# Keys of the neighbourhood heads kept on both sides of the context's keys, with two score matmuls per block

## The chip, the cores and the metric

The kernel runs on one core of a Trainium2 chip. The metric is the device time of one execution in microseconds (us). The engines are PE (TensorE: matmuls, with PEld for its weight loads), DVE (VectorE), ACT (ScalarE), POOL (GpSimd) and SP (SyncE, which issues most DMAs).

## The reference

One layer of a diffusion backbone over 512 latent tokens (a grid of 8 rows by 64 columns) and 256 context tokens, width 1024, everything in fp32. The layer has a modulated norm, one input projection, two groups of 8 attention heads each, an output projection with a gated residual, a mixture of 16 experts, and a last norm. The change lies in the second group, the neighbourhood heads (64 wide). Each latent query sees the keys of a window of 8 by 16 grid positions, with a learned bias for each relative position, and all 256 context keys, in one softmax:

```python
s = jnp.einsum('bqhd,bjkhd->bhqjk', qr, kr).astype(jnp.float32) * scale
s = s + jnp.transpose(bias, (0, 2, 1, 3)).astype(jnp.float32)[None]
s = jnp.where(col_in[None, None, :, None, :], s, MASK_VALUE).reshape(B, H, GRID_W, kh * GRID_W)
s_ctx = jnp.einsum('bqhd,bchd->bhqc', qr, k_ctx).astype(jnp.float32) * scale
p = jax.nn.softmax(jnp.concatenate([s, s_ctx], axis=-1), axis=-1).astype(v.dtype)
```

## The kernel before, in words

The latent tokens are laid out column of the grid by column, so that a window of 16 columns is 128 neighbouring tokens, a tile. The queries are shifted by 64 tokens against the keys: a block of 128 queries needs two key tiles. Query blocks i = 0, 1 and 2 need key tiles i and i + 1; block 3, which holds both ends of the grid, needs tiles 3 and 0. Each block has 512 scores for each query: 256 of latent keys and 256 of context keys.

The heads are worked on in four pairs, p = 0 to 3, with u = 0, 1 for the head in the pair and i = 0 to 3 for the block: 32 blocks, numbered b (line 712). The keys of a head lie in the tile `kk`, 128 partitions by 768 columns: columns 0 to 511 are the four latent tiles, 512 to 767 the context. Partitions 0 to 63 hold the key rounded to fp32r, 64 to 127 the rest that rounding leaves. The queries have two operands, `qh` (rounded, twice) and `ql` (the rest), so a score is two fp32r matmuls on the same columns, added up in PSUM. The functions around the change are these.

- `na_bias` (lines 548 to 552): DVE writes two biases with their masks into `bb`, one for blocks 0 to 2 and one for block 3, whose first half is for tile 3 and second for tile 0.
- `na_part` (lines 575 to 589): brings a projection out of PSUM. For keys, ACT copies to the upper half of `kk` (line 587) and DVE subtracts into the lower half (line 589). j = 1 is the latent keys, j = 2 the context's.
- `na_scores` (lines 593 to 606): the score matmuls, lines 604 (`qh`) and 605 (`ql`). Blocks 0 and 1 have two pieces of 256 columns (window, context), four matmuls. In block 2 the tiles 2 and 3 lie next to the context, so it has one piece of 512, two matmuls. Block 3 has pieces of 128, 128 and 256 columns, six matmuls.
- `na_max` (lines 608 to 611): DVE adds the bias to the window's 256 columns in PSUM (line 610) and takes the row maximum (line 470).
- `na_exp` (lines 613 to 617): ACT's exponential with row sums.
- `na_turn` (lines 619 to 627): four transposes on PE, copied to `pt` by DVE or ACT in turn (lines 82 and 84).
- `na_values` (lines 629 to 651): the product with the values; its rows of 512 columns take their moving operand from `pt` in four runs of 128 columns.

The loop over the blocks (lines 712 to 775) writes out the order by hand: scores, maximum, one step of the next pair's projections (`pull`, lines 57 to 59), the transposes of the block before, the exponential, after every second block a part of the modulation (`mod_rest`, line 521: two loads of 512 KB of `w_mod_b` on SP's queue into three `raw` buffers, and eight matmul instructions), and more steps of the projection, counted in `NS`. In the last pair the projections pulled are those of the latent attention (values, and splits of its weights), which come through the same `raw` buffers. The framework that builds the program may put an instruction ahead of earlier ones of its engine that are not ready yet, so the order in the trace is not quite that of the text. After this stage come the latent attention and then the experts.

Of the kernel before, what the change touches and what calls it, by code (L numbers as in the profile page):

```python
# [13 lines left out]
OP = mybir.AluOpType  # L14
# [3 lines left out]
P = 128  # L18
D = 1024
KT = 8  # L20
T = 512
TC = 256
# [11 lines left out]
K_MA, K_MB, K_KC, K_KS, K_QC, K_QS = 0, 256, 512, 640, 768, 896  # L34
# [4 lines left out]
def hybrid_kernel(tc, nc, x_k, x_q, ctx, cvec, w_mod_a, w_mod_b, b_mod_c, b_mod_r, g_ffn_row,  # L39
                  w_v, w_kv, w_ql, w_qk, g_q, g_kv, w_uq, w_ukv, rel, w_out_a, w_out_b, w_r, b_r,  # L40
                  w_gate, w_up, w_down, g_fin_row, cpk0, cpk, out):
    sy, ac, ve, pe, gp = nc.sync, nc.scalar, nc.vector, nc.tensor, nc.gpsimd
# [7 lines left out]
    def f(ap):  # L50
        return ap.bitcast(F32)
# [27 lines left out]
    def copy(dst, src, of=2):  # L79
        turn[0] += 1  # L80
        if turn[0] % of == 1:
            ve.tensor_copy(dst, src)
        else:
            ac.copy(dst, src)
# [34 lines left out]
    ident = c0[:, C_ID:C_ID + P]  # L119
# [53 lines left out]
    cka = htp.tile([P, K_QC], F32, name="cka")  # L173
# [28 lines left out]
    def bank(*nums):  # L202

        n = taken[nums] = taken.get(nums, -1) + 1
        return psA.tile([P, 512], F32, name="ps", tag=f"b{nums[n % len(nums)]}", bufs=1)

    def bank4(*nums):
        return bank(*nums).rearrange("p (a b) -> p a b", a=4)
# [143 lines left out]
    for b in range(3):  # L352
        n = KB[b + 1] - KB[b]
        wh, wl = load_split(w_kv[:, KB[b] * 288:KB[b + 1] * 288], n * 288)
        for i in range(n):
            k = KB[b] + i
            s = slice(i * 288, (i + 1) * 288)
            for t in range(6):
                mm3(akv[t][:, 0:288], hh[:, k, key_cols(t)], hl[:, k, key_cols(t)], wh[:, s], wl[:, s],
                    start=(k == 0), stop=(k == KT - 1))  # L360
# [4 lines left out]
    for b in range(4):  # L365
        wh, wl = load_split(w_ql[b], 768)
        for i in range(2):
            k = 2 * b + i
            s = slice(i * 384, (i + 1) * 384)
            for t in range(4):  # L370
                mm3(aq[t][:, 0:384], hh[:, k, q_cols(t)], hl[:, k, q_cols(t)], wh[:, s], wl[:, s],
                    start=(k == 0), stop=(k == KT - 1))
# [16 lines left out]
    ks = cka[:, K_KS:K_KS + 128].rearrange("p (t d) -> p t d", t=4)  # L389
# [5 lines left out]
    for c in range(2):  # L395
        for b0, n in ((0, 4), (4, 2)):
            tr = bank4(4, 5, 6)
            for i in range(n):
                pe.transpose(tr[:, i, :], kvt[:, b0 + i, c * P:(c + 1) * P], ident)
            s = slice(b0 * P, (b0 + n) * P)  # L400
# [4 lines left out]
    for b0, n in ((0, 4), (4, 2)):  # L405
        tr = bank4(4, 5, 6)
# [10 lines left out]
    for c in range(3):  # L417
        tr = bank4(4, 5, 6)
# [48 lines left out]
    def row_max(s):  # L467

        nm = cst.tile([P, 1], F32, name="nm", tag="nm", bufs=8)
        ve.tensor_reduce(out=nm, in_=s, axis=AX.X, op=OP.max, negate=True)  # L470
        return nm
# [76 lines left out]
    def na_bias(p, u):  # L548

        *_, bb, rb = na_heads[p][u]  # L550
        ve.tensor_tensor(bb[:, 0, :], rb, cka[:, K_MA:K_MA + 256], op=OP.add)
        ve.tensor_tensor(bb[:, 1, :], rb, cka[:, K_MB:K_MB + 256], op=OP.add)

    def na_weights(p, j, i):

# [19 lines left out]
    def na_part(p, j, u, i):  # L575

        qh, ql, kk, *_ = na_heads[p][u]
        n, dst = ((T, 0), (T, 0), (TC, T))[j]
        pu = na_ps[p, j][u * 64:u * 64 + 64, 0:n]
        if j == 0:  # L580
            if i == 0:
                for o in range(2):
                    ac.activation(qh[o * 64:o * 64 + 64, :], pu, AF.Copy, scale=0.125)
            else:
                ve.scalar_tensor_tensor(ql[0:64, :], pu, 0.125, f(qh[0:64, :]), op0=OP.mult, op1=OP.subtract)
        elif i == 0:
            ac.copy(kk[0:64, dst:dst + n], pu)
        else:
            ve.tensor_tensor(kk[64:128, dst:dst + n], pu, f(kk[0:64, dst:dst + n]), op=OP.subtract)

    na_pts, na_ssum, na_pr = {}, {}, {}

    def na_scores(p, u, i):
        qh, ql, kk, *_ = na_heads[p][u]
        qs = slice(i * P, (i + 1) * P)
        s = bank(2, 3)
        if i == 2:
            pieces = ((0, 512, 256),)
        elif i == 3:
            pieces = ((0, 128, 384), (128, 128, 0), (256, 256, 512))  # L600
        else:
            pieces = ((0, 256, i * P), (256, 256, 512))
        for o, n, c in pieces:
            pe.matmul(s[:, o:o + n], qh[:, qs], kk[:, c:c + n], start=True, stop=False)
            pe.matmul(s[:, o:o + n], ql[:, qs], kk[:, c:c + n], start=False, stop=True)
        return s

    def na_max(p, u, i, s):
        bb = na_heads[p][u][3]
        ve.tensor_tensor(s[:, 0:256], s[:, 0:256], bb[:, 1 if i == 3 else 0, :], op=OP.add)  # L610
        return row_max(s)

    def na_exp(p, u, i, s, nm):
# [5 lines left out]
    def na_turn(p, u, i):  # L619

        if i == 0:
            na_pts[p, u] = nw.tile([P, 4, 4, P], F32, name="pt", tag="pt", bufs=2)
        pr = na_pr.pop((p, u, i))
        tr = bank4(4, 5)
        for j in range(4):
            pe.transpose(tr[:, j, :], pr[:, j * P:(j + 1) * P], ident)  # L626
        copy(na_pts[p, u][:, i], tr)

    def na_values(p):
# [64 lines left out]
    for j in range(3):  # L694
        for n, _ in enumerate(na_project(0, j)):
            if n == 0 and j:
                for u in range(2):
                    na_part(0, j - 1, u, 0)
                    na_part(0, j - 1, u, 1)
            if n == 4 and j == 1:  # L700
                na_weights(1, 0, 0)
                na_weights(1, 0, 1)

                ac.activation(sm[:, 20:21], f(kvo[:, 1, T + TC - 1:T + TC]), AF.Exp, scale=0.0)
                for u in range(2):
                    na_bias(0, u)
    pull(PF)
    for u in range(2):
        na_part(0, 2, u, 0)
        na_part(0, 2, u, 1)  # L710
    turns = []
    for b, (p, u, i) in enumerate(blocks):
        w = b % 8
        if w == 0 and p < 3:
            na_open(p + 1)
        s = na_scores(p, u, i)
        nm = na_max(p, u, i, s)
        if p < 3:
            if w in (3, 5, 7):
                for u_ in range(2):  # L720
                    na_part(p + 1, w // 2 - 1, u_, 1)
            if w == 2:
                na_weights(p + 1, 1, 1)
            if w == 4 and p < 2:
                na_weights(p + 2, 0, 1)
            if w == 6:
                for u_ in range(2):
                    na_bias(p + 1, u_)
        if NS[p][w] > 1:
            pull(1)  # L730
        if len(turns) >= (2 if b > 24 else 1):
            na_turn(*turns.pop(0))
# [43 lines left out]
    for tn in turns:  # L776
        pull(1)
        na_turn(*tn)
# [146 lines left out]
    def mla_scores(h, t):  # L925
        qh, ql = qhl[h]
        kh, kl = khs[h % NK], kls[h % NK]
        qs = slice(t * P, (t + 1) * P)
        s = big()
        for a, b in ((0, T), (T, T + TC)):  # L930
            mm3(s[:, a:b], qh[0:96, qs], ql[0:96, qs], kh[0:96, a:b], kl[0:96, a:b], start=True, stop=True)
        return s[:, 0:768]
# [88 lines left out]
    for b, (h, t) in enumerate(blocks):  # L1021
        p, w = divmod(b, 8)
        s = mla_scores(h, t)
# [627 lines left out]
    with tc.manual_schedule(engines={pe.engine, ve.engine, ac.engine}):  # L1651
# [19 lines left out]
        for n in range(8):  # L1671
            wh, wl = half(n)
            for i in range(2):
# [3 lines left out]
                    start=(k == 0), stop=(k == KT - 1))  # L1677
# [233 lines left out]
```

## Time and profile before

| what | value |
|---|---|
| median of 3 runs | 737.57 us (736.07 to 739.32) |
| the profiled execution | 736.98 us, of which its span is 735.2 us |
| mean granted PE clock over the span | 0.985 of full speed |
| PE busy | 699.1 us, 95% of the span |
| DVE, ACT, POOL busy | 546.2, 447.2, 83.4 us |

The span runs from the first to the last instruction; what lies around it is 1.8 us. A busy PE counts the time from a matmul's start to its modelled end, so matmuls overlap in it: what a matmul costs is read from the distance to the next one, which the chain of waits gives.

### The profile page before, as it was taken

The numbers are of one execution on the slowest core, as the hardware profiler recorded it, in microseconds if no ns is written. First come the engines' busy times: TensorE is split into PE (matmuls) and PEld (weight loads), VectorE is DVE, ScalarE is ACT, GpSimd is POOL, SyncE is SP. The second block draws the span as 40 slices with busy tenths as digits, with TensorE's granted clock in tenths as the row PEclk, the third lists the DMA queues.
The fourth block names the chain that finished last, engine by engine and source line by source line (L and its number), as shares of the span: only waits on it lengthen the run. The fifth ranks groups of instructions, "written<-read, shape, count | busy, mean of one in ns | idle before, by whom it ended". The sixth has DMA issues, their size and how long they took to land.

```text
span 735.2 us, 10575 instructions
## 1 busy us (share of the span) xinstructions
PE 699.1 (95%) x3982; PEld 520.7 (71%) x3983; DVE 546.2 (74%) x741; ACT 447.2 (61%) x698; POOL 83.4 (11%) x56
## 2 busy tenths in 40 slices
PE   4999999999999999999999779999999999999995
PEld 3678988777765787868668657777777777777773
DVE  5572456666666695766536778999999999999996
ACT  6451354554555464646654377777777777777763
POOL 1010000000000000000010111222222222221320
PEclk9999999999999999999999969999999999999998
DMA  8931238555466831021269969999999999999572
GB/s 322 409 118 58 72 108 274 183 175 185 143 202 229 269 95 58 31 94 48 72 218 383 336 218 397 351 377 372 370 364 365 364 359 353 350 351 374 199 132 114
DMA packets 39335, 174.57 MB, mean 237 GB/s; under 512 B 5711, under 2 KB 7191, under 8 KB 26992
## 3 DMA queue, kind: packets, MB, share of 16 engines
q1 hardware_dynamic: 34880, 163.72, 61.3%
q0 software_dynamic: 4112, 10.06, 6.2%
q8 instruction: 32, 0.52, 0.3%
q14 instruction: 23, 0.19, 0.1%
q10 hardware_dynamic: 288, 0.08, 0.0%
HBM read 163.00 MB, written 14.79 MB: 242 GB/s over the span
## 4 chain that ended last, share of the span: by engine, by line
PE 89%; DMA 4%; DVE 3%; ACT 2%; issue 1%; SPq 0%; DVEq 0%; ACTq 0%
PE s L57 11%; PE s L59 11%; PE s L58 11%; PE ps L57 6%; PE ps L59 6%; PE ps L58 6%; PE y L59 4%; PE y L57 4%; PE y L58 4%; PE o L960 3%; PE tr L951 3%; PE ps L521 2%; PE ps L635 2%; DMA raw<-w_mod_b 2%; PE t L1511 1%; PE ps L626 1%
## 5 line engine op out<-in xcount | busy, mean ns | idle before, releaser
L1368 DVE TENSOR_TENSOR el<-ew,eh 128x2048 fp32r<-128x2048 f32 (+1 forms) x106 | 220.6, 2087 | 16.6 <-ACT eh L1365 13.6
L1365 ACT CAST eh<-ew 128x1024 fp32r<-128x1024 f32 x190 | 189.7, 1048 | 43.6 <-PE s L59 29.0
L57 PE MATMUL s<-eh,xh 128*96 128x512 f32 x260 | 104.5, 402 | 0.9 <-ACT xh L62 0.9
L59 PE MATMUL s<-eh,xl 128*96 128x512 f32 x260 | 103.1, 396 | 0.0
L58 PE MATMUL s<-el,xh 128*96 128x512 f32 x260 | 102.5, 394 | 0.0
L1580 POOL DMA_INDIRECT ya_d<-yo,idx x14 | 45.5, 3251 | 140.3 <-DVE yo L1584 140.3
L59 PEld LDWEIGHTS s<-eh,xl 128*96 128x96 f32 x260 | 42.2, 162 | 19.2 <-DVE xl L63 0.6
L57 PEld LDWEIGHTS s<-eh,xh 128*96 128x96 f32 x260 | 42.3, 163 | 18.0 <-ACT xh L62 1.2
L58 PEld LDWEIGHTS s<-el,xh 128*96 128x96 f32 x260 | 42.5, 163 | 17.4 <-DVE el L1368 0.2
L57 PE MATMUL y<-eh,ghh 128*96 128x512 f32 x120 | 48.1, 401 | 0.0
L59 PE MATMUL y<-eh,ghl 128*96 128x512 f32 x120 | 47.3, 394 | 0.0
L58 PE MATMUL y<-el,ghh 128*96 128x512 f32 x120 | 47.2, 393 | 0.0
L470 DVE TENSOR_REDUCE nm<-s 128x1 f32<-128x768 f32 x32 | 30.5, 954 | 19.4 <-PE s L59 19.1
L57 PE MATMUL ps<-wh,hh 128*128 128x512 f32 (+2 forms) x128 | 43.8, 345 | 0.4 <-ACT hh L275 0.3
L59 PE MATMUL ps<-wh,hl 128*128 128x512 f32 (+2 forms) x128 | 43.5, 345 | 0.2 <-DVE hl L277 0.2
L58 PE MATMUL ps<-wl,hh 128*128 128x512 f32 (+2 forms) x128 | 43.4, 341 | 0.0
L1295 POOL MEMSET xg<- 128x1024 f32 x2 | 1.9, 960 | 326.1 <-PE s L59 326.1
L57 PE MATMUL ps<-hh,wh 128*128 128x512 f32 (+1 forms) x96 | 36.4, 380 | 0.0
L938 ACT ACTIVATE pr<-s,nm 128x768 f32<-128x768 f32 x32 | 29.0, 908 | 9.8 <-DVE nm L470 9.3
L59 PE MATMUL ps<-hh,wl 128*128 128x512 f32 (+1 forms) x96 | 34.4, 358 | 0.0
L58 PE MATMUL ps<-hl,wh 128*128 128x512 f32 (+1 forms) x96 | 34.1, 356 | 0.0
L617 ACT ACTIVATE pr<-ps,nm 128x512 f32<-128x512 f32 x32 | 22.1, 690 | 15.8 <-DVE nm L470 15.7
(360 smaller groups left out, 1476.9 us busy)
## 6 DMA issues: line engine op xcount, KB each, us to landing
ew<-w_gate SPq DMA_DIRECT2D x32, 1024.0 KB, 8.6
ew<-w_up SPq DMA_DIRECT2D x32, 1024.0 KB, 8.3
ew<-w_down SPq DMA_DIRECT2D x32, 1024.0 KB, 8.8
raw<-w_mod_b SPq DMA_DIRECT2D x32, 512.0 KB, 4.0
wm<-w_mod_a SPq DMA_DIRECT2D x16, 512.0 KB, 10.8
raw<-w_qk SPq DMA_DIRECT2D x8, 512.0 KB, 3.5
raw<-w_v SPq DMA_DIRECT2D x4, 512.0 KB, 9.6
ya_d<-zero SPq DMA_DIRECT2D x8, 256.0 KB, 3.3
```

The source lines that it names most:

```text
L57: pe.matmul(ps, lh, rh, start=start, stop=False)
L58: pe.matmul(ps, lh, rl, start=False, stop=False)
L59: pe.matmul(ps, ll, rh, start=False, stop=stop)
L470: ve.tensor_reduce(out=nm, in_=s, axis=AX.X, op=OP.max, negate=True)
L521: pe.matmul(ps[g * 32:(g + 1) * 32, :], sstat[:, k, :], ws[g // 2][:, g % 2 * 512:g % 2 * 512 + 512], start=(k == 0), stop=(k == KT - 1), ...
L617: ac.activation(pr, s, AF.Exp, bias=nm, accum_out=na_ssum[p][:, i, u:u + 1])
L938: ac.activation(pr, s, AF.Exp, bias=nm, accum_out=mla_ssum[h // 2][:, t, h % 2:h % 2 + 1])
L951: pe.transpose(tr[:, n % 4, :], pr[:, j * P:(j + 1) * P], ident)
L960: pe.matmul(o[u * 64:u * 64 + 64, :], vv[:, j, h * 64:h * 64 + 64], mla_pts[h][:, :, j, :], start=(j == 0), stop=(j == 5), tile_position=( ...
L1365: ac.copy(wh[:, cs], r[:, cs])
L1368: ve.tensor_tensor(wl[:, cs], r[:, cs], f(wh[:, cs]), op=OP.subtract)
L1580: gp.indirect_dma_start(out=ya_d, out_offset=bass.IndirectOffsetOnAxis(ap=idx[rows, 1, e:e + 1], axis=0), in_=yo[rows, :], in_offset=None, ...
```

## The change

The latent key tiles 0 and 1 stay in columns 0 to 255 of `kk`, tiles 2 and 3 move to columns 512 to 767, and the context's keys move to columns 256 to 511 between them. Blocks 0, 1 and 2 then take 512 neighbouring columns from column 128 i on; block 3 takes tile 0, both context tiles and tile 3, in runs of 128 columns that start at columns 0, 256, 384 and 640, as one operand with gaps. Each block has two matmuls of 512 columns. The window's scores then lie at other columns of the block's PSUM bank: the bias is added to two runs of 128 columns in blocks 1 and 3, the bias of block 3 is written with its halves swapped, by two DVE instructions, and the transposes take their tiles in the order `NA_AT`.

```diff
-        ve.tensor_tensor(bb[:, 1, :], rb, cka[:, K_MB:K_MB + 256], op=OP.add)
+
+        for o in (0, P):
+            ve.tensor_tensor(bb[:, 1, P - o:2 * P - o], rb[:, o:o + P], cka[:, K_MB + o:K_MB + o + P], op=OP.add)
...
-        n, dst = ((T, 0), (T, 0), (TC, T))[j]
+        n = (T, T, TC)[j]
         pu = na_ps[p, j][u * 64:u * 64 + 64, 0:n]
+
+        kv_ = kk.rearrange("p (a b) -> p a b", b=TC)[:, 0:3:2, :] if j == 1 else kk[:, None, TC:2 * TC]
+        pv_ = pu.rearrange("p (a b) -> p a b", b=TC)
...
-            ac.copy(kk[0:64, dst:dst + n], pu)
+            ac.copy(kv_[0:64], pv_)
         else:
-            ve.tensor_tensor(kk[64:128, dst:dst + n], pu, f(kk[0:64, dst:dst + n]), op=OP.subtract)
+            ve.tensor_tensor(kv_[64:128], pv_, f(kv_[0:64]), op=OP.subtract)
...
-        if i == 2:
-            pieces = ((0, 512, 256),)
-        elif i == 3:
-            pieces = ((0, 128, 384), (128, 128, 0), (256, 256, 512))
+        if i < 3:
+            ks = kk[:, i * P:i * P + 512]
         else:
-            pieces = ((0, 256, i * P), (256, 256, 512))
-        for o, n, c in pieces:
-            pe.matmul(s[:, o:o + n], qh[:, qs], kk[:, c:c + n], start=True, stop=False)
-            pe.matmul(s[:, o:o + n], ql[:, qs], kk[:, c:c + n], start=False, stop=True)
+            ks = kk.rearrange("p (a b c) -> p a b c", a=2, b=3)[:, :, 0:3:2, :]
+        pe.matmul(s, qh[:, qs], ks, start=True, stop=False)
+        pe.matmul(s, ql[:, qs], ks, start=False, stop=True)
         return s
+
+
+    NA_AT = ((0, 1, 2, 3), (0, 3, 1, 2), (2, 3, 0, 1), (3, 0, 1, 2))
...
-        ve.tensor_tensor(s[:, 0:256], s[:, 0:256], bb[:, 1 if i == 3 else 0, :], op=OP.add)
+        st = s.rearrange("p (a b) -> p a b", b=P)
+        sw = (st[:, 0:2], st[:, 0:4:3], st[:, 2:4], st[:, 0:4:3])[i]
+        ve.tensor_tensor(sw, sw, bb[:, 1 if i == 3 else 0, :].rearrange("p (a b) -> p a b", b=P), op=OP.add)
...
-            pe.transpose(tr[:, j, :], pr[:, j * P:(j + 1) * P], ident)
+            o = NA_AT[i][j] * P
+            pe.transpose(tr[:, j, :], pr[:, o:o + P], ident)
```

## Rows read from the trace of the kernel before

**Rows 1.** The page: busy time by engine; the chain that ended last, by engine.

```profile
PE 699.1 (95%) x3982; PEld 520.7 (71%) x3983; DVE 546.2 (74%) x741; ACT 447.2 (61%) x698; POOL 83.4 (11%) x56
...
PE 89%; DMA 4%; DVE 3%; ACT 2%; issue 1%; SPq 0%; DVEq 0%; ACTq 0%
```

**Rows 2.** Busy time by stretch: length, engines, then PE clock, DMA share, GB/s.

```profile
122.00:201.40 79.40, 79.40 (x534) 58.26 (x533) 51.62 (x93) 41.40 (x86) 0.00 (x0) 1.00 0.54 178
201.40:245.00 43.60, 40.76 (x268) 25.94 (x269) 27.21 (x48) 21.53 (x47) 0.00 (x0) 1.00 0.65 205
440.00:700.00 260.00, 260.00 (x1241) 185.06 (x1240) 245.59 (x159) 199.56 (x223) 66.10 (x27) 1.00 0.97 352
```

**Rows 3.** The chain, 201 to 228 us: start, us, what it was.

```profile
201.41 0.28 SPq L180
...
201.78 6.73 DMA raw<-w_ukv
...
217.54 3.88 DMA raw<-w_mod_b
...
222.56 4.93 DMA raw<-w_mod_b
```

**Rows 4.** Line 604 over the span (line 605 has the same forms).

```profile
L604 PE MATMUL ps<-kk,qh x64: 222/281/476, 121.7 to 233.0; 128*128 128x256 f32 x40, 128*128 128x128 f32 x16, 128*128 128x512 f32 x8
```

**Rows 5.** The chain, block 3 of the first head, 0 and 2 of the second.

```profile
129.53 0.06 PE ps L604
129.59 0.11 PE ps L605
129.71 0.11 PE ps L604
129.82 0.11 PE ps L605
129.93 0.17 PE ps L604
130.10 0.12 PE ps L605
...
133.91 0.12 PE ps L604
...
141.12 0.23 PE ps L604
...
141.59 0.12 PE ps L57
```

**Rows 6.** Timeline of PE: the first matmul of block 23 (head 6, block 3).

```profile
204.77 0.22 PE L604 MATMUL ps<-kk,qh 128*128 128x128 f32 x1
```

**Rows 7.** Groups by form, 112 to 236 us: busy, mean ns, idle before.

```profile
L610 DVE TENSOR_TENSOR ps<-ps,bb 128x256 f32<-128x256 f32 x32 | 13.7, 430 | 18.5 <-PE ps L605 18.0
L552 DVE TENSOR_TENSOR bb<-rb,cka 128x256 f32<-128x256 f32 x8 | 3.3, 410 | 0.0
```

**Rows 8.** Line 838, a DVE multiplication that reads PSUM in runs of 32 columns.

```profile
L838 DVE TENSOR_TENSOR q<-s,ckq x8: 273/288/292, 250.1 to 263.4; 128x128 f32<-128x128 f32 x8
```

**Rows 9.** Timeline at the start of the second pair: last key subtraction, first score.

```profile
144.34 0.88 DVE L589 TENSOR_TENSOR kk<-ps,kk 64x256 fp32r<-64x256 f32 x2 [1.56 <-ACT kk L587]
...
146.98 0.28 PE L604 MATMUL ps<-kk,qh 128*128 128x256 f32 x1
```

**Rows 10.** Groups by form: fp32 matmuls with a whole and a broken moving operand.

```profile
L521 PE MATMUL ps<-raw,sstat 128*32 128x512 f32 x124 | 19.1, 605 | 0.7 <-DMA raw<-w_mod_b 0.7
...
L635 PE MATMUL ps<-pt,nav 128*64 128x512 f32 x24 | 8.3, 605 | 0.0
```

**Rows 11.** The chain: eight instructions of line 521, fp32.

```profile
131.34 0.99 PE ps L521 x8
```

**Rows 12.** Timeline of PE in block 0: a projection before the second piece.

```profile
121.91 0.40 PE L57 MATMUL ps<-hh,wh 128*128 128x512 f32 x1
...
122.37 0.37 PE L604 MATMUL ps<-kk,qh 128*128 128x256 f32 x1
```

## The prediction

> **What bounds the kernel now.** I read the page first. PE is busy 95% of the span and holds 89% of the chain that ended last, so a shorter PE stretch shows in the time wherever nothing else takes the chain over [rows 1]. The busy times by stretch say where that holds. From 122 to 201.4 us, where the first three pairs of neighbourhood heads run, PE is busy for all of its 79.4 us; DVE is busy 51.6 and ACT 41.4 of them, the clock is full and the DMA engines are at 0.54 [rows 2]. That stretch is PE's own, and PE time taken out of it comes off its end. From 201.4 to 245 us PE has holes (40.8 of 43.6), and the chain runs over loads: SP issues the load of `w_ukv` at 201.41, its landing takes 6.73 us, and later two landings of `w_mod_b` take 3.88 and 4.93 [rows 3]. PE work saved there waits for the same landing. After that comes work that starts when this stage ends; the experts keep PE busy 260.0 of 260 us [rows 2], so what is gained before them should arrive at the end undiminished.
>
> **PE: the score matmuls.** Line 604 has 64 matmuls, 40 of 256 columns, 16 of 128 and 8 of 512, and line 605 as many [rows 4]: 16 for each of 8 heads. The busy times overlap, so I take distances along the chain. The two matmuls of 512 columns of a block 2 take 0.47 (from 141.12 to the next line at 141.59), 0.235 each. One of 256 takes 0.12 (133.91), so the four of block 0 or 1 take 0.48. The six of block 3, from 129.53 on, take 0.06 + 0.11 + 0.11 + 0.11 + 0.17 + 0.12 = 0.68 [rows 5]. A head costs 0.48 + 0.48 + 0.47 + 0.68 = 2.11 before and 4 x 0.47 = 1.88 after: 0.23 saved, of which 0.21 is block 3's. Blocks 0 and 1 had as many columns before as after and give 0.01 each; block 2 gives nothing.
>
> Why block 3 is the dear one can be read from the same rows. A matmul of 512 columns runs at 0.235 / 512 = 0.46 ns a column, and 128 columns at that rate are 0.06 us. The first piece of 128 takes that, the next three take 0.11: the pieces are too short to cover something that comes with each matmul, most likely the load of its 128 columns of weights. The Trainium skill has this twice over. Its page "TensorE: Matmul & The Clock Gate", section "LDWEIGHTS (loading the stationary operand)", gives columns / 1.2 ns, 107 ns for 128 columns, and with that the trace agrees (0.11). The same page's section "Back-to-back issue gap" gives, for matmuls by themselves, columns / 2.4 + 2.5 ns; by that rule alone a matmul taken away is worth 2.5 ns, and the 64 taken away 0.16 us in all, a time of 736.8.
>
> How much of it lies on the path: SP's issue at 201.41 falls before block 23, whose first matmul is at 204.77 [rows 6]. So five of the block 3s and twelve of the blocks 0 and 1 lie in PE's own stretch: 5 x 0.21 + 12 x 0.01 = 1.17. The other three block 3s lie among the loads and I count them at nothing; their cover is the landings of rows 3, and without it they are worth 3 x 0.21, some 0.6 more. **Bounds: 0 to 8 x 0.23 = 1.84 saved; I take 1.2.**
>
> **DVE: two bias instructions for one.** The 256 columns take 0.410 [rows 7]. A DVE product of two tensors on 128 columns takes 0.288 [rows 8], so two take 0.58, 0.17 more per head, 1.3 us over all heads. They are issued in the sixth block of a pair, ahead of the maximum of the next block, which ACT's exponential and PE's transposes of that block wait for. DVE has 18.0 us in which it waits for PE's scores [rows 7], so it catches up before PE notices: 0. If that cover is gone, three pairs lose 2 x 0.17 each, 1.0 us. A gain is excluded, as the same columns are done with more instructions.
>
> **Runs with gaps on DVE and ACT.** The bias addition in blocks 1 and 3 works on two runs of 128 in PSUM; contiguous it takes 0.430 [rows 7]. The nearest row reads PSUM in runs of 32 and takes no more than an addition of its size should: 0.288, where 0.430 less 128 of its columns at about 1 ns is 0.30 [rows 7, 8]. So I take 0. The upper end is two instructions in place of one, 2 x 0.288 - 0.430 = 0.15, on DVE and under the same cover, half of it on the path at worst (16 blocks, 1.2 us). The copies into `kk` move as many elements as before in two runs; ACT and DVE have a third of the stretch free or more [rows 2], and I take 0 for them too. The transposes read other columns of the same tile: nothing.
>
> **The wait for the context's keys.** Before, the first piece of a pair's block 0 can start without the context's keys; now the first matmul needs all of `kk`. In the second pair the last subtraction into `kk` starts at 144.34 and with its fellow takes 0.88, to 145.22; the first score is at 146.98, 1.76 later [rows 9]. Only in the very first block did the second piece come later than the first, and there PE did projections in between [rows 12]. So 0; at most the 0.24 of the two matmuls that could start early, once a pair, 1.0 in all. No DMA is added, removed or moved past another in the text.
>
> **The sum.** 736.98 (span 735.2 and 1.8 around it) less 1.2 is 735.8. The median of the runs, 737.57, is 0.6 above the profiled execution, and from it the sum is 736.4. I put the forecast midway, 736.1.
>
> **The rivals.** (1) *No gain*: 737.0. The pieces would stream at 0.46 ns a column whatever their length, block 3 would have cost 0.47 already, or its operand with gaps is issued in pieces again, or DVE's additions take back what PE gives. Against it: rows 5 show the 0.11, and DVE's idle time. The page's issue gap, above, is the rule for it. 0.16.
>
> (2) *A load falls behind in the last pair, slower*. The order on each engine isn't just the text's: in block 0 a projection slipped in ahead of the second piece [rows 12]. With two matmuls where four or six stood, the framework may place line 521 or a projection differently in the last pair, and PE then stands before a load with the scores queued behind it. Place: 201 to 245 us, where landings are already the chain. Price: one more landing, 3.88 to 4.93 [rows 3], less 1.2: 739.7 to 740.7. It decides as soon as the added wait is over 1.2. Against it: the order by hand is unchanged and the DMA engines are at 0.65 [rows 2]. 0.09.
>
> (3) *A load gets ahead there*, by the same shuffling: 1.2 and 3.88 to 4.93, so 730.9 to 731.9. 0.08.
>
> (4) *The operand with gaps drops to the speed of plain fp32*. Eight instructions of line 521 are four such products side by side and take 0.99 [rows 11]; two after one another would make block 3 cost 1.98, not 0.68, and 5 x 1.30 less 0.12 makes 743.4. It decides once block 3 costs more than 0.68. Against it: fp32 matmuls with a moving operand in four runs of 128 take 605 ns, to the ns what those with a whole operand take [rows 10], so gaps as such cost PE nothing. 0.03.
>
> **How the numbers follow.** The forecast has the remaining 0.64. Half a per cent of 737.6 is 3.7 us, about what a measurement of this kernel can tell from no change: under 733.9 is faster, over 741.3 slower. Faster: rival 3, and 0.03 of the forecast's own spread: 0.11. Slower: rival 4, and 0.03 of rival 2, whose upper end lies near the bound: 0.06. Same: 0.83. The range takes in the forecast with its bounds (1.84 saved, or 1.0 to 1.2 lost on DVE and still 736.98 at most), rival 1, and about 1 us that runs of one kernel differ from their median: 733.5 to 739.3. It leaves out rivals 2, 3 and 4, 0.20.
>
> **What would show it.** Lines 604 and 605 with 32 matmuls each, all of 512 columns, 0.235 apart in the chain, in block 3 as in the others; 64 PE matmuls fewer; the first pairs' stretch, from 122 us to SP's issue of `w_ukv`, shorter by 1.2; line 552's successor with 16 instructions near 0.29; DVE's wait for line 605 about as long as now; the end of the stage 1 to 1.5 earlier, and everything after it in the same order and as long as now. The forecast is wrong if block 3's matmuls are over 0.3 us apart, if the landings after 201 us are other in number or length, or if the stage ends over 3 us from where it should.

## The result and the profile after

| | before | changed |
|---|---|---|
| median, 13 executions each | 737.66 us (735.42 to 740.76) | 734.52 us (733.54 to 736.23) |
| ratio, 95% interval | | 0.995 [0.9935, 0.9965] |
| the profiled execution | 736.98 us, span 735.2 | 733.54 us, span 731.8 |

The changed kernel is faster by 3.1 us by the medians, 2.6 to 4.8 by the interval. The forecast of 736.1 was 1.6 us too high and its range held the time; its 1.2 us of gain are less than half of what came. The ratio lies on the line of half a per cent that the prediction drew between faster and no change. The page of the changed kernel, against [rows 1]:

```profile
span 731.8 us, 10466 instructions
...
PE 698.1 (95%) x3918; PEld 516.9 (71%) x3919; DVE 546.4 (75%) x749; ACT 447.7 (61%) x698; POOL 83.7 (11%) x56
...
PE 41%; DVE 1%; ACT 0%; DVEq 0%; issue 0%; ACTq 0%
```

PE has the 64 matmuls fewer (3982 to 3918), DVE 8 instructions more, and PE's busy time fell by 1.0 us only, since busy times of neighbouring matmuls overlap. The chain breaks off here in the experts (its shares add up to 42%), so what lies ahead of them is read from stretches and the timeline. Groups by form, 112 to 236 us, against [rows 4] and [rows 7]:

```profile
L617 DVE TENSOR_TENSOR ps<-ps,bb 128x256 f32<-128x256 f32 x32 | 13.7, 430 | 20.1 <-PE ps L607 19.9
L606 PE MATMUL ps<-kk,qh 128*128 128x512 f32 x32 | 13.2, 412 | 0.0
L607 PE MATMUL ps<-kk,ql 128*128 128x512 f32 x32 | 12.8, 398 | 0.0
...
L554 DVE TENSOR_TENSOR bb<-rb,cka 128x128 f32<-128x128 f32 x16 | 4.0, 282 | 0.0
```

The scores are 32 + 32 matmuls of 512 columns. The bias addition, half of whose blocks now read two runs of 128 from PSUM, still takes 430 ns. The bias of block 3 takes two instructions of 282 ns, and DVE waits longer for the scores than before (19.9 us against 18.0), not shorter. The timeline of PE in block 3 of the first head, against the first six lines of [rows 5]:

```profile
129.63 0.39 PE L606 MATMUL ps<-kk,qh 128*128 128x512 f32 x1
129.86 0.39 PE L607 MATMUL ps<-kk,ql 128*128 128x512 f32 x1
130.09 0.39 PE L57 MATMUL ps<-hh,wh 128*128 128x512 f32 x1
```

From 129.63 to 130.09 is 0.46 us, where six matmuls took 0.68: the operand with gaps runs like any other. Busy time by stretch, against [rows 2]:

```profile
122.00:200.60 78.60, 78.60 (x492) 55.69 (x491) 52.32 (x99) 41.35 (x86) 0.00 (x0) 1.00 0.55 180
200.60:241.40 40.80, 40.26 (x248) 24.06 (x249) 27.05 (x48) 21.72 (x47) 0.00 (x0) 1.00 0.65 214
```

The first stretch is still PE's own from end to end. What no step of the forecast had is in the second: it lost 2.8 us of length (43.6 to 40.8), while PE's holes in it went from 2.84 to 0.54 us. The longest waits say which holes. PE's waits from 200 to 260 us (us in all, times, longest), before:

```profile
PE ps L57 <- ACT wh L62: 1.5, 1, 1.5
PE ps L521 <- DMA raw<-w_mod_b: 1.3, 4, 0.6
```

and in the changed kernel:

```profile
PE ps L521 <- DMA raw<-w_mod_b: 0.5, 1, 0.5
```

The wait of 1.5 us for the first weights of `w_ukv` is gone. On the timeline before, the split of those weights on ACT begins at 208.54, 6.76 us after SP issued their load (201.78), and PE goes on at 209.21:

```profile
208.54 0.62 ACT L62 CAST wh<-raw 128x512 fp32r<-128x512 f32 x1 [2.75 <-DMA raw<-w_ukv]
...
209.21 0.49 PE L57 MATMUL ps<-wh,kvh 128*128 128x512 f32 x1 [1.50 <-ACT wh L62]
```

In the changed kernel it begins 4.97 us after the issue, and PE waits for nothing:

```profile
200.96 0.38 SPq L180 DMA_DIRECT2D raw<-w_ukv  x1
...
205.93 0.62 ACT L62 CAST wh<-raw 128x512 fp32r<-128x512 f32 x1 [0.96 <-DMA raw<-w_ukv]
...
206.60 0.50 PE L57 MATMUL ps<-wh,kvh 128*128 128x512 f32 x1
```

What else the DMA engines did in the two landings is in the DMA view (queue: packets, MB, share of 16 engines). Before, 201.7 to 208.6 us:

```profile
q1 hardware_dynamic: 494, 1.34, 67.6%
q8 instruction: 1, 0.02, 0.9%
```

In the changed kernel, 200.9 to 206 us, there is one line only:

```profile
q1 hardware_dynamic: 466, 1.27, 77.4%
```

Queue 8 carries instructions, in 32 packets of 16 KB over the whole span. One of them fell into the load before (at 205.0 us) and not after (at 210.7). In the microsecond from 204.6 on it took 6.0% of 16 engines, 0.96 us of one. The trace also has the times of the sixteen signals that tell of the load's end. Before, fifteen of them are there 4.79 us after the issue and the last only after 6.74; in the changed kernel the fifteenth comes after 4.79 too and the last after 4.95.

The second difference is the order at the end of the stage, on the timeline of PE before:

```profile
238.56 1.05 PE L521 MATMUL ps<-raw,sstat 128*32 128x512 f32 x4 [0.64 <-DMA raw<-w_mod_b]
239.54 0.55 PE L626 MATMUL ps<-c,pr 128*128 128x128 f32 x3
240.71 4.03 PE L635 MATMUL ps<-pt,nav 128*64 128x512 f32 x40
244.67 0.66 PE L486 MATMUL ps<-c,rsb 128*128 128x128 f32 x4
```

and in the changed kernel:

```profile
234.26 0.60 PE L634 MATMUL ps<-c,pr 128*128 128x128 f32 x4
235.48 1.07 PE L643 MATMUL ps<-pt,nav 128*64 128x512 f32 x2
236.48 1.05 PE L521 MATMUL ps<-raw,sstat 128*32 128x512 f32 x4
237.47 3.68 PE L643 MATMUL ps<-pt,nav 128*64 128x512 f32 x38
241.07 0.66 PE L486 MATMUL ps<-c,rsb 128*128 128x128 f32 x4
```

Before, the last four instructions of line 521 stood in front of the last three transposes and waited 0.64 us for their load, so the copies and values behind them were late too. In the changed kernel the framework puts them behind the transposes and the first values, and their load is there. The text of the kernel has the same order in both.

### The profile page after: what moved, and what is told of

Its sections match the earlier page's. It is cut to its first block, busy times and chain, and to the rows that moved or that the text cites. A ratio compares the mean times of both kernels' runs of the same rounds, so it can differ in the third digit from the quotient of the medians.

```text
span 731.8 us, 10466 instructions
## 1 busy us (share of the span) xinstructions
PE 698.1 (95%) x3918; PEld 516.9 (71%) x3919; DVE 546.4 (75%) x749; ACT 447.7 (61%) x698; POOL 83.7 (11%) x56
## 5 line engine op out<-in xcount | busy, mean ns | idle before, releaser
L1261 POOL DMA_INDIRECT xg<-hx_d,idx x16 | 24.2, 1510 | 65.9 <-PE t L1519 46.7
## 6 DMA issues: line engine op xcount, KB each, us to landing
raw<-w_v SPq DMA_DIRECT2D x4, 512.0 KB, 10.5
```

Source lines behind the costliest of these rows:

```text
L1261: ins = gp.indirect_dma_start(out=xg[e % NX][slice(0, CAP), :], out_offset=None, in_=hx_d, in_offset=bass.IndirectOffsetOnAxis(ap=idx[slic ...
```

## The experiments

One execution of each kernel was profiled. The profiled executions differ by some 2 us before the neighbourhood heads begin, and the time of one kernel scatters by 3 to 7 us, more than the effects sought. So the table goes by distances on the timeline, in us: **M** is the first matmul of line 521 (124.17 us before, 124.40 after); "issue" is SP's issue of `w_ukv`; "landing" the time from there to the first split on ACT; "wait" what PE then waits for it; "packet" the start of the instruction packet near it, and whether it lies inside the landing; "stage" the start of the last four matmuls of line 486 in this stage (in the changed kernel 241.07); "latent" the same at the end of the latent attention; "rest" from there to the end of the span.

| kernel | issue - M | landing | wait | packet | stage - M | latent - M | rest |
|---|---|---|---|---|---|---|---|
| before | 77.61 | 6.76 | 1.50 | 205.0, inside | 120.50 | 259.47 | 351.6 |
| changed | 76.56 | 4.97 | 0 | 210.7, outside | 116.67 | 255.45 | 351.9 |
| e1 before again | 77.60 | 6.81 | 1.55 | 203.8, inside | 120.29 | 259.23 | 351.6 |
| e2 all pieces | 77.58 | 6.73 | 1.47 | 205.2, inside | 120.86 | 259.78 | 352.8 |
| e3 merge first | 76.56 | 5.29 | 0.20 | 208.9, outside | 117.33 | 256.11 | 354.8 |
| e4 before, tail | 77.57 | 6.86 | 1.59 | 205.3, inside | 118.36 | 258.18 | 351.6 |
| e5 before, padded | 77.59 | 5.00 | 0 | 198.7, outside | 118.74 | 257.71 | 354.7 |
| e6 changed, padded | 76.56 | 6.82 | 1.76 | 204.0, inside | 120.04 | 258.81 | 354.4 |
| e7 changed, old tail | 76.56 | 5.01 | 0 | 209.1, outside | 117.96 | 256.70 | 351.9 |
| e8 block 3 twice | 78.55 | 4.94 | 0 | 211.6, outside | 120.56 | 259.30 | 355.5 |
| e9 changed again | 76.50 | 4.89 | 0 | 210.5, outside | 116.57 | 255.38 | 353.2 |
| e10 padded, store first | 76.56 | 6.91 | 1.83 | 204.5, inside | 118.50 | 257.35 | 353.0 |
| e11 changed, tail | 76.56 | 4.93 | 0 | 211.0, outside | 114.72 | 254.45 | 354.3 |
| e12 e11, store first | 76.76 | 4.90 | 0 | 210.6, outside | 114.70 | 254.45 | 352.7 |

Three groups of four kernels ran on one chip each, beside the kernel before (medians 737.03, 737.47 and 737.38 us), with 10 to 12 executions of each of the four.

### e1: the kernel before, unchanged

> The kernel before, unchanged. Both theories: ratio 1.000 within 0.1%. What it tells apart is the load of w_ukv issued at 201.8 us, whose landing took 6.73 us in the profile of before and 4.94 in that of after, and for which PE stood still 1.5 us in the one and not in the other. If that is the order of the work, the landing takes 6 to 7 us again, PE waits 1 to 2 us for L62 and the stage ends at 244.7 within 0.5. If it is chance of the transfers, the landing may take about 5 and the stage ends some 1.5 earlier.

737.39 us, ratio 1.0006 [0.9987, 1.0024]. From M on, the timeline repeats to 0.3 us (its first two columns to 0.05), though M itself came 1.2 us earlier. So differences of more than 0.3 us in the table are read as the kernel's, those in the time are not. The last column is no such measure: between the two profiles of the changed kernel (e9) it differs by 1.3 us.

### e2: the new layout with the old pieces

```diff
+        if i != 2:
+            if i == 3:
+                pieces = ((0, 128, 0), (384, 128, 640), (128, 256, 256))
+            else:
+                pieces = ((0, 256, i * P), (256, 256, i * P + 256))
+            for o, n, c in pieces:
+                pe.matmul(s[:, o:o + n], qh[:, qs], kk[:, c:c + n], start=True, stop=False)
+                pe.matmul(s[:, o:o + n], ql[:, qs], kk[:, c:c + n], start=False, stop=True)
+            return s
```

> The new layout of the keys with the pieces of before: the matmuls are those of before, DVE has its 8 additions more and the two-run bias additions. If the layout and DVE cost nothing, the issue of w_ukv stays at 201.8 within 0.3 and the ratio is 1.000 within 0.15%. If DVE's additions reach the path, up to 1.0 us more, 1.0014. If the gain of the change came from the layout and not from the matmuls, 0.996.

738.4 us, ratio 1.0014 [0.9995, 1.0033]. Everything but the merged matmuls is in it: the keys in two runs, the swapped bias in two instructions, additions and transposes on other columns. The issue is 0.03 us from that of the kernel before, and the packet and the wait are the old ones. So the gain hangs on the number of matmuls, and DVE's and ACT's part of the change costs nothing up to the issue. The stage ends 0.36 us later, and PE waits 0.6 us longer there for loads of `w_mod_b` (1.9 us in all against 1.3). The time alone would not have told: its interval also takes in the 1.0014 that was named for a loss on DVE.

### e3: two matmuls in the first three pairs, pieces in the last

```diff
+        if p == 3 and i != 2:
...
```

> Two matmuls per block in the first three pairs, pieces in the last; PE's order in the tail of the last pair is that of before. Theory of block 3 alone: the issue of w_ukv comes 1.05 us earlier (five block 3s at 0.21), and the time falls by 1.05 to 1.3, ratio 0.9984. If the landing of w_ukv is also shortened by what happens before it, 1.7 more, 0.996. If all of the 3.1 us came evenly from the merged matmuls, six heads of eight give 2.4, 0.9968.

735.5 us, ratio 0.9975 [0.9957, 0.9993]. The first three pairs give 1.05 us, as in the changed kernel, and the landing is short here too (5.29). The last four instructions of line 521 stand in front of the last three transposes, as before, but don't wait. With the last pair in pieces as before and the old tail, the latent attention ends 0.66 us later than in the changed kernel and 3.36 earlier than before: most of the gain in the last pair comes from what the first three do.

### e4: the kernel before with its tail turned by hand

```diff
+        if n == 15:
+            products(range(2))
+            held.extend((lambda: products((2, 3)), close))
+        else:
+            products(range(4))
...
         norm_.send((na_values(3), bank4(4, 5)))
+        for step in held:
+            step()
```

`products` is the four matmuls of line 521; the last four of all now stand behind the values.

> The kernel before, with the second half of the last modulation part (four matmul instructions of line 521, which wait for the last load of w_mod_b) placed behind the last product with the values in the text; its load is issued where it was. Theory that PE's order in the tail gave 1.5 us of the gain: the stage ends 1.5 to 2.5 earlier than 244.7, ratio 0.998 or below. Rival, that the end of the stage hangs on ACT and DVE and not on that wait: no change, 1.000 within 0.1%.

735.16 us, ratio 0.997 [0.9947, 0.9993]. On PE the values now end the stage, and the four come after it:

```profile
239.01 3.90 PE L645 MATMUL ps<-pt,nav 128*64 128x512 f32 x40
242.84 0.66 PE L486 MATMUL ps<-c,rsb 128*128 128x128 f32 x4
243.43 1.05 PE L522 MATMUL ps<-raw,sstat 128*32 128x512 f32 x4
```

With the load of `w_ukv` as slow as ever (6.86), the stage ends 2.14 us earlier, of which 1.29 is left at the end of the latent attention, since the four matmuls still have to be done. The order at the tail is worth something without any change to the scores.

### e5 and e6: the instruction packet moved by padding

```diff
+    idle = bank(7)
+    for _ in range(18):
+        pe.matmul(idle[0:32, 0:1], sstat[:, 0, :], sstat[:, 0, 0:1], start=True, stop=True)
```

18 products of one column, in fp32 and so 36 matmuls and 36 weight loads in the trace, go to the very start (1.3 to 3.2 us), in e5 of the kernel before and in e6 of the changed one. They touch nothing that is used.

> The kernel before with 18 tiny fp32 products (72 PE records in the trace) on zeros at the very start, where PE has nothing to do; the order on every engine is otherwise that of before. In all profiles so far a 16 KB packet of instructions is fetched when PE starts about its 2769th record; before that is at 205.0 us, inside the load of w_ukv (landing 6.7 to 6.9 us in four profiles), with the change at 210.7 or 208.9, after it (5.0 and 5.3). Theory that the packet delays the load: with 72 records in front it comes at about 200.3, ahead of the load, the landing takes about 5, PE's wait of 1.5 is gone and the stage is 1.4 to 1.7 shorter from its first L521 on; ratio 0.998. Rival, that the landing depends on the order of the work: 6.8 us again, ratio 1.000.

> The changed kernel with the same 72 PE records at the start, order otherwise unchanged. Theory of the packet: it moves from 210.7 to about 204.5 us, into the load of w_ukv; the landing takes 6.5 to 7 us in place of 5.0, PE waits 1 to 1.6 us, and of the gain of 3.1 us about 1.5 is gone: ratio 0.997. Rival: landing 5.0, ratio 0.995 as without them.

On the timeline both went as far as the landing is concerned. In e5 the packet came at 198.7, ahead of the issue, and the kernel before had the short landing (5.00) and no wait of PE for it:

```profile
202.29 0.38 SPq L180 DMA_DIRECT2D raw<-w_ukv  x1
...
207.29 0.62 ACT L62 CAST wh<-raw 128x512 fp32r<-128x512 f32 x1 [1.00 <-DMA raw<-w_ukv]
```

Its stage ended 1.76 us earlier, without any change to the scores or their order. In e6 the packet came at 204.0, inside, and the changed kernel had the long landing (6.82) and the wait back:

```profile
200.77 0.38 SPq L180 DMA_DIRECT2D raw<-w_ukv  x1
...
207.59 0.62 ACT L62 CAST wh<-raw 128x512 fp32r<-128x512 f32 x1 [2.83 <-DMA raw<-w_ukv]
...
208.27 0.49 PE L57 MATMUL ps<-wh,kvh 128*128 128x512 f32 x1 [1.76 <-ACT wh L62]
```

Its stage ended 3.37 us later than the changed kernel's: 1.76 is the wait, and behind it the clock fell, as told in the last section. In e10, with the same packet and a full clock, the stage ends 1.83 us later, which is its wait.

The times did not follow: e5 took 738.97 us, ratio 1.0024 [1.0003, 1.0044], where 1.76 us less were due; e6 took 738.09, ratio 0.9997 [0.9977, 1.0017]. In both profiles the rest behind the latent attention is 2.5 to 3.1 us longer than without the padding. So the padding shows what the packet does in this stage; what else padding does to the time is open (e10).

### e7: the changed kernel with the old tail

```diff
+            if (p, u, i) == (3, 1, 3) and j > 0:
+                behind(ins)
...
+    def behind(ins, of=None):
+        tc.add_manual_dep(ins.ins, (of or last)[0], mybir.DependencyInfo(
+            mybir.DependencyClass.NoSync, mybir.DependencyReason.DATA), reason="order")
...
+            if p == 3:
+                behind(ins)
```

It holds the last three transposes and the last pair's values behind line 521's last matmul, by order alone.

> The changed kernel with PE held, in the tail of the last pair, to put the last four matmul instructions of line 521 (which wait for the last load of w_mod_b) ahead of the last three transposes, the products with the values and the last normalisation, as before. Theory that this part of the order is worth about 1 us: the stage ends 0.7 to 1.5 later than with the change, ratio 0.9965. Rival, that it is worth nothing since the load lands early: 0.995.

734.8 us, ratio 0.9974 [0.9951, 0.9997], which takes in both expected values. Stage and latent attention end 1.29 and 1.25 us later than in the changed kernel; the four instructions wait longer than they did before, as all of PE's work is earlier and their load is not:

```profile
234.81 1.05 PE L523 MATMUL ps<-raw,sstat 128*32 128x512 f32 x4 [1.35 <-DMA raw<-w_mod_b]
```

### e8: block 3's two matmuls done twice in the first three pairs

```diff
-        pe.matmul(s, qh[:, qs], ks, start=True, stop=False)
-        pe.matmul(s, ql[:, qs], ks, start=False, stop=True)
+        for _ in range(2 if i == 3 and p < 3 else 1):
+            pe.matmul(s, qh[:, qs], ks, start=True, stop=False)
+            pe.matmul(s, ql[:, qs], ks, start=False, stop=True)
```

> The changed kernel with the two score matmuls of block 3 done twice in the first three pairs. If PE is the bound there and they take 0.47, the stretch from the first L521 to the issue of w_ukv grows by 5 x 0.47 = 2.35 against the change (76.6 to 78.9) and the time by 2.4 to 2.8. If something else has come to bound the stretch, it grows by under 1. If block 3's operand with gaps were slower than 0.47, by more than 2.6.

739.32 us, ratio 1.0015 [0.999, 1.004]. The timeline of PE in block 3:

```profile
129.34 0.39 PE L607 MATMUL ps<-kk,qh 128*128 128x512 f32 x1
129.57 0.40 PE L608 MATMUL ps<-kk,ql 128*128 128x512 f32 x1
129.80 0.39 PE L607 MATMUL ps<-kk,qh 128*128 128x512 f32 x1
130.03 0.39 PE L608 MATMUL ps<-kk,ql 128*128 128x512 f32 x1
130.26 0.39 PE L57 MATMUL ps<-hh,wh 128*128 128x512 f32 x1
```

All four are 0.23 apart. Five blocks ahead of the issue moved it by 1.99 us, 0.40 each where two matmuls take 0.46: nearly all that PE does more in this stretch comes out at its end, and rival 4 is excluded by a direct measurement. The later end of the stage is not all from there: at 222.6 us PE waits 1.6 us for a load of `w_mod_b` in this run.

### e9 to e12: the changed kernel again, the expert start, and the two edits together

e9 is the changed kernel, unchanged. e10 is e6, and e12 is e11, with the store of the last rows of `hx_d`, which the experts gather from, issued on SP ahead of a load of `w_up` that stood before it. e11 is the changed kernel with e4's tail.

```diff
-        load_experts(L2 - 1)
         tile_end(3, s3)
-        load_experts(1)
+        load_experts(L2)
```

> The changed kernel, unchanged, beside the three that follow. Ratio 0.995 to 0.997. In its profile the landing of w_ukv takes about 5 us with the instruction packet near 210, as before; from the last L486 of the latent attention to the end of the span 351.5 to 352 us if the store of the last rows goes well behind the w_up load (over 0.45 us), 354 to 355 if it goes out right behind it (0.38).

> The changed kernel with the 72 PE records at the start, and the store of the last token rows (hx_d) ahead of the w_up load in SP's queue in place of behind it. In four profiles that took 354 to 355.5 us from the last L486 of the latent attention to the end, the store went out 0.38 to 0.71 us behind that load and the first gather came 10.1 to 11.1 after it; in those that took 351.5 to 352.8 the gather came 6.9 to 8.4 after it. If the load ahead of the store is the cause, the gather comes under 8.5 us after the store and the rest takes 351 to 352.5: the time falls by about 2 to 3 us against the padded kernel (738.1), ratio 0.996. If it is not, 354 again and 0.9995.

> The changed kernel with the second half of the last modulation part placed behind the last product with the values, as in the run of the kernel before with that edit (whose stage was 2.1 us shorter, the latent attention's end 1.3 earlier). With the change PE no longer waits for that load, only does its four instructions (1.0 us) ahead of the values: 0.5 to 1.0 us less, ratio 0.994. If the end of the stage hangs on the transposes' copies and not on PE, no difference from the unchanged one beside it.

> Both edits on the changed kernel, without the records at the start: 0.5 to 1.0 from the tail, and the store ahead of the load. In profiles of the quick kind the store's place is worth little (0 to 0.7), so 1 us less than the changed kernel and fewer runs near 736: ratio 0.993. If the load that now comes later is missed by the first expert, up to 1 us is lost again.

| | us | ratio |
|---|---|---|
| e9 | 735.17 | 0.9974 [0.9955, 0.9993] |
| e10 | 737.99 | 1.001 [0.9991, 1.0029] |
| e11 | 734.0 | 0.9954 [0.9939, 0.9969] |
| e12 | 734.32 | 0.997 [0.9951, 0.9989] |

e9 repeats the stage of the changed kernel to 0.1 us, while its time against before came out at 2.2 us less here and 3.1 there: that is how far the time alone can be trusted. e10 was to test whether the padded kernels lose their gain at the start of the experts. In e6 the store goes right behind a load of `w_up`, and the first gather comes 10.5 us after the store:

```profile
416.43 0.33 SPq L458 DMA_DIRECT2D ew<-w_up  x1
416.81 0.42 SPq L1262 DMA_DIRECT2D hx_d<-t  x1
...
427.31 1.08 POOL L1265 DMA_INDIRECT xg<-hx_d,idx  x1 [5.43 <-DVEq L1419]
```

In the changed kernel the store has 0.8 us behind the load, and the gather follows after 7.3:

```profile
412.75 0.33 SPq L454 DMA_DIRECT2D ew<-w_up  x1
413.55 0.33 SPq L1258 DMA_DIRECT2D hx_d<-t  x1
...
420.82 1.09 POOL L1261 DMA_INDIRECT xg<-hx_d,idx  x1 [2.14 <-DVE ex L1166]
```

With the store first, the gather came 6.9 us after it in e10 and e12 and the rest was 353.0 and 352.7 us, shorter than in e6 (354.4) and e11 (354.3), by 1.4 and 1.6 us, which is little more than the 1.3 between e9 and the changed kernel. The times did not get better for it (e10 against e6, e12 against e11): e10's time is the one expected if that load is not the cause (0.9995), and e12 missed its 0.993. And e9 has the store 0.38 us behind the load, as close as e6, with its gather after 7.7. So the distance alone does not decide; what makes the rest of the program 351.6 to 353.2 us in some executions and 354.3 to 355.5 in others, of either kernel's layout, stays open. The place is known: the experts' first matmul comes 47.8 to 49.9 us after the end of the latent attention in the first kind and 50.9 to 52.0 in the second, and from it to the end of the span it is 302.9 to 304.3 us in all 14.

e11 ends the stage 1.95 us and the latent attention 1.00 us earlier than the changed kernel, and has the lowest median of the study, 1.2 us under the changed kernel beside it. The intervals of e9 and e11 overlap, so that e11 is the better of the two is likely and not shown.

## Why the prediction was right, and where it was short

**PE bounds the first three pairs, and block 3 is the dear one: right.** The stretch from M to the issue is 1.05 us shorter in the changed kernel, in e3, e6, e7, e10 and e11 (77.6 to 76.56; 76.50 in e9 and 76.76 in e12), where the sum had 1.17. It equals 5 x 0.21, the five block 3s alone; whether the 12 x 0.01 of blocks 0 and 1 is there, such a scatter can't tell. That short pieces cost 0.11 us each was read correctly from [rows 5]. The Trainium skill's rule in "TensorE: Matmul & The Clock Gate", section "Back-to-back issue gap", makes the 44 matmuls taken out of this stretch worth 44 x 2.5 ns, 0.11 us by estimate; the trace has 1.05, so the rule, which that section gives for isolated matmuls, is not the one that counts where every matmul brings its own weights.

**DVE, the runs with gaps, the wait for the context's keys: right at nothing.** e2 has the first two and the stretch is the old one; the additions take 430 ns as before, the two bias instructions 282 ns each (0.288 forecast). e2 doesn't have the third, as its first piece still takes latent keys alone; there the changed kernel itself tells, in whose first stretch PE has no hole (78.60 busy of 78.60 us).

**The failed step: "The other three block 3s lie among the loads and I count them at nothing; their cover is the landings of rows 3".** The stage ended 3.83 us earlier, not 1 to 1.5, and the gain of 3.1 us in the medians is above even the upper bound of the sum, 1.84. The prediction had named the sign by itself: landings after 201 us of another length. I took 6.73 us as what that load takes. (The prediction dates its issue 201.41; that is SP's issue of a load of `w_mod_b` just ahead of it, and that of `w_ukv` is at 201.78. Nothing hangs on it.) The load takes 5 us, and the rest was a disturbance: a packet of PE's own instructions. In all 14 profiles it starts when PE has begun 2716 to 2748 matmuls and weight loads, those of the padding included. With 44 matmuls fewer by the issue it comes later, 5.7 us later in the profile, and misses the load. In all 14 profiled executions the landing is 6.7 to 6.9 us where the packet lies inside it (before, e1, e2, e4, e6, e10) and 4.9 to 5.3 where it doesn't (the other eight), and padding moved it both ways (e5, e6). It is worth 1.76 us here (e5; 1.83 in e10). The sixteen signals of the load say how: the fifteenth comes 4.8 to 5.0 us after the issue in all 14 profiles, and the last 1.9 to 2.0 us behind it where the packet lies inside and at most 0.4 where it doesn't. So, as far as the signals tell, one part in sixteen of the load is held up, and ACT's split begins only behind the last signal (208.52, then 208.54 before). In the changed kernel it does the same to a load that PE does not wait for: the one of `w_mod_b` issued at 208.70 has its last signal 1.40 us behind the fifteenth. Why a packet of 0.96 us costs that part up to twice as much is not shown. This part of the gain is luck: the edit was not made for it, and 72 records more at the start, matmuls and weight loads, take it back (e6).

**The other new term is the last pair itself: 1.2 us.** At the end of the latent attention the gain is 4.02 us; 1.05 for the first pairs and 1.76 for the packet leave 1.2. e7 lays all of it to the order at the tail (1.25), but its forced order brought a wait of 1.35 us with it; e3, with the old order and the pieces, lost only 0.66. How much of the 1.2 is order and how much the three block 3s (3 x 0.21), counted at nothing, is not settled. e4 shows that the order alone has such a price, 1.29 with a stronger edit.

**The rivals.** Rival 3, a load that gets ahead in the last pair, given 0.08, happened together with the forecast. Its cause was only half there: the framework did reorder the tail, but the greater part came through instruction packets, of which [rows 3] shows only the effect. Its price, a whole landing of 3.88 to 4.93 us, was too high: 1.76 and 1.2. Rival 2 had the same place with the other sign, and e6 shows that 18 tiny products are enough to bring the wait back. Rivals 1 and 4 fell with e2, e3 and e8.

**From the stage to the end.** 4.02 us at the end of the latent attention are 3.63 at the end of the span, both counted from M (735.2 - 124.17 against 731.8 - 124.40), and 3.1 in the medians. "Undiminished" was nearly right in these two profiles; e3, e5, e6, e8 and e11 show that up to 3 us can be lost ahead of the experts' first matmul; the cause is open.

## What to carry to other kernels

Where PE bounds and each matmul brings its own 128 columns of weights, merge pieces of 128 columns, if need be as one moving operand with gaps: 512 columns cost 0.23 us either way, a piece of 128 costs 0.11. Don't take one landing in one profile for the length of a load: look in the DMA view for an instruction packet inside it, and know that an edit that changes PE's count of instructions can move the packets against the loads. Give small gains by distances on the timeline from a common event, since the time of one kernel scatters by more, and look at the order at a stage's tail, which may change without a change of the text.

## What was not expected of the hardware

An instruction packet of 16 KB, some 1 us of one DMA engine, makes the landing of `w_ukv` 1.8 us longer when it falls into that load: one of the load's sixteen end signals comes 1.9 to 2.0 us behind the others. The Trainium skill, in "Runtime: NRT & Kernel Launch", section "Instruction fetch mechanics", says that instructions are refilled in blocks of 16 KiB over a DMA queue and calls the cost of crossing a block's boundary "mostly hidden". The trace agrees with the size (16,384 bytes a packet); PE's stream shows no stop at the packet here, but the load of `w_ukv` beside it came later.

After the same stop of PE the clock may fall or not. In e6 PE stood for 1.76 us and in e10 for 1.83, in the same place of nearly the same kernel. Busy time by stretch around it (length, engines, clock, DMA share, GB/s), in e6:

```profile
206.50:208.50 2.00, 0.24 (x2) 0.19 (x1) 1.00 (x3) 0.91 (x2) 0.00 (x0) 1.00 0.70 185
208.50:212.80 4.30, 4.30 (x13) 2.12 (x12) 2.11 (x5) 2.53 (x6) 0.00 (x0) 0.60 0.75 284
```

and in e10:

```profile
207.00:209.00 2.00, 0.30 (x1) 0.19 (x1) 0.96 (x2) 0.97 (x2) 0.00 (x0) 1.00 0.74 206
209.00:213.20 4.20, 4.20 (x29) 2.46 (x29) 3.46 (x8) 3.32 (x9) 0.00 (x0) 1.00 0.73 280
```

In e6 the granted clock fell to half, 1.2 GHz, for 3.4 us behind the stop (0.60 over the 4.3 us), and PE did 13 matmul instructions in that time, where in e10 it stayed at 2.4 GHz and PE did 29. The latent attention ended 1.46 us later in e6 than in e10. One wait of 1.8 us can thus cost 1.8 or 3.3 us, by something that these runs don't show.
